# Attention core: in every second step one copy out of PSUM goes from VectorE to ScalarE

## The chip, the core and the metric

The kernel runs on one core of one Trainium2 chip. Its engines take part under the profile's names: PE is TensorE (matrix products, and transposes as products with the identity), PEld its weight loads, DVE is VectorE, ACT is ScalarE, POOL is GpSimd, SP issues transfers. The metric is the device time of one execution in microseconds (us); less is better.

## The reference, cut to what is computed

A backbone of two layers over 1024 latent tokens and 256 context tokens, width 1024. Layer 0 mixes with a Fourier transform and a state-space scan, layer 1 with differential attention; each layer ends in a squared-ReLU MLP. The change lies in the attention of layer 1, which has 8 heads, two score maps per head, and keys and values over all 1280 tokens:

```python
def diff_attend(q, k, v, lam):
    s = jnp.einsum("bqhmd,bkhmd->bhmqk", q, k).astype(F32) * (DA_HEAD_DIM ** -0.5)
    p = jax.nn.softmax(s, axis=-1)
    w = (p[:, :, 0] - lam * p[:, :, 1]).astype(v.dtype)
    return jnp.einsum("bhqk,bkhd->bqhd", w, v)
```

Queries are taken in blocks of 128 tokens, so that there are 8 heads times 8 blocks.

## The kernel before

Everything is in 32-bit floats. `attn_core` works through 64 items, one for each head and each block of 128 queries (`qt` counts the blocks). It is a software pipeline written out by hand: the loop over `i` issues in one step the work of up to five items at different stages, and every engine runs its own instructions in the order in which they are written. The names of the stages are those of the code: in step `i`, `cur` is item `i`, `last` is item `i-1`, `turned` is item `i-2`, `old` is item `i-3` and `done` is item `i-4`.

For item `cur`, `qk` (line 2002) computes on TensorE the scores of the first map into the PSUM tile `SC[0]` and of the second map into `SC[1]`, 128 x 1280 each, in six products each. `peak` (line 2007) takes each row's maximum on VectorE, `expo` (line 2013) the exponential with the row's sum on ScalarE, into the SBUF tiles `P` and `R`. For `last`, `combine` and `combine_tail` form first map plus factor times second map: VectorE makes the reciprocal (line 2020) and the factor, GpSimd the first 896 columns, VectorE the last 384. For `turned`, `turn` (lines 2033 to 2038) transposes the ten 128 x 128 tiles of the combined weights on TensorE through the PSUM tile `TB`, which holds four of them: first the tiles 8 and 9, then 4 to 7, then 0 to 3. After each of the three groups `TB` is copied into the SBUF tile `wT`. For `old`, `pv` (line 2042) multiplies the transposed weights with the values. For `done`, `store` scales the result and `power` (line 2051) takes its sum of squares.

There is one `TB`, one `SC[0]` and one `SC[1]`: `qk` of the next step overwrites what `expo` of this step reads. In a step TensorE's order is: scores of the first map, transposes 8 and 9, scores of the second map, transposes 4 to 7, half of `pv`, the other half, transposes 0 to 3. ScalarE's order is: copy 8 and 9, `power`, copy 4 to 7, first exponential, second exponential. VectorE's order is: reciprocal and factor, `store`, both maxima, tail of the combination, small operations from a list (`drip`, at most three in a step), copy 0 to 3.

Once per head, the output rows are normalized: `norm` puts some dozen small operations on the list, which lie in the steps with a number of 4 to 7 modulo 8, and `out` transposes the results through `TB` (four more transposes in steps with the number 0 and 1 modulo 8, with a copy by ScalarE, line 2085, and a cast by VectorE, line 2086, one step later). Towards the end of the core, splits of weight tiles (lines 349 and 353) are put behind the steps as well. Helpers such as line 312 and 340 record the operations of many places in the code, so that the tile's name tells which one it is.

Of the kernel before, what the change touches and what calls it, by code (L numbers as in the profile page):

```python
# [217 lines left out]
class Kern:  # L218
# [1763 lines left out]
    def attn_core(self, P, rest, more, tail):  # L1982
# [3 lines left out]
        p0r, p1r, s2 = P  # L1986
        cols = [(0, 512), (512, 512), (1024, 256)]
        f = lambda a: a.rearrange("p a b -> p (a b)")
        heads, items = self.heads, {}

        def begin(h, qt):
            if qt == 0:
                O = self.R.v(8, 128) if h + 1 < NH else self.Kr.v(8, 128).bitcast(F32)
                heads[h].update(O=O, t=s2.v(4, 8))
            it = items[h, qt] = dict(st=self.S.v(2, 8), P=[p0r.v(1280)])
            return it

        def qk(h, qt, i, part):
# [30 lines left out]
        def turn(it, c0):  # L2029
            m = min(4, 10 - c0)  # L2030
            ps = self.TB[:, :128 * m]
            for j in range(m):
                nc.tensor.transpose(ps[:, 128 * j:128 * j + 128],  # L2033
                                    it["P"][0][:, 128 * (c0 + j):128 * (c0 + j) + 128], self.ident)
            if c0:
                nc.scalar.copy(f(it["wT"][:, c0:c0 + m]), ps)
            else:
                nc.vector.tensor_copy(f(it["wT"][:, c0:c0 + m]), ps)
# [53 lines left out]
        for i in range(n + 5):  # L2092
# [5 lines left out]
            if cur:  # L2098
                h, qt = cur
                if i == 2:  # L2100
                    self.core_q(0, 1)
                if h + 1 < NH:
                    if qt == 3:
                        self.core_load(h + 1)
                    if qt == 4:
                        self.core_q(h + 1, 0)
                    if qt == 6:
                        self.core_q(h + 1, 1)
                it = begin(*cur)
                qk(*cur, 0, cols)  # L2110
                peak(it, 0)
            if turned:
                ti = items[turned]
                ti["wT"] = wr.v(10, 128)
                turn(ti, 8)
# [4 lines left out]
            if turned:  # L2120
                turn(ti, 4)
# [18 lines left out]
            if turned:  # L2140
                turn(ti, 0)
# [358 lines left out]
```

## Time and profile before

| | |
|---|---|
| time, median of 3 runs | 2878.57 us (2871.09 to 2879.25) |
| the profiled execution | 2877.97 us, span of its trace 2876.2 us |
| TensorE busy (PE) | 2782.5 us, 97% of the span |
| its weight loads (PEld) | 2327.5 us, 81% |
| VectorE busy (DVE) | 2030.6 us, 71% |
| ScalarE busy (ACT) | 1132.2 us, 39% |
| GpSimd busy (POOL) | 1517.7 us, 53% |
| copies of line 2038 (DVE) | 64, of 677 to 693 ns, from 1745.3 to 2123.9 us |
| copies of line 2036 (ACT) | 128, 64 of 256 columns and 64 of 512, of 372 to 587 ns |

The shares are means over stages that have different limits. Times in the views of the trace count from the span's start.

### The profile page before, as it was taken

Reading aid. Unit: us, or ns where it says so; the run is one execution under the profiler, and the core shown is the slowest. Engines: PE = TensorE matmul, PEld = TensorE weight load, DVE = VectorE, ACT = ScalarE, POOL = GpSimd, SP = SyncE. Lnnn points to the kernel's source line nnn. Section 1 sums busy time; section 2 is a strip of 40 time slices with the busy share of each in tenths; the row PEclk is TensorE's granted clock in tenths of the full one; section 3 lists DMA queues with packets and bytes.
Section 4 is the critical chain, followed back from the end, with each engine's and each line's share of the span. In section 5 each row is a group of like instructions: output and inputs, shape, how many; then the busy total and the mean of one; then the engine's idle time right before and its main releaser. Section 6 shows DMA issues by size and latency. Waiting matters only on the chain. (4 is left out here: it accounts for less than half of the span.)

```text
span 2876.2 us, 40633 instructions
## 1 busy us (share of the span) xinstructions
PE 2782.5 (97%) x14850; PEld 2327.5 (81%) x14850; DVE 2030.6 (71%) x3769; ACT 1132.2 (39%) x2036; POOL 1517.7 (53%) x1247
## 2 busy tenths in 40 slices
PE   5899999999999999999999999999999999999999
PEld 2666788788888888888778788999988888878887
DVE  7789867785654566668588848999977344347776
ACT  3341434444444311113334436666643545432220
POOL 5613313544444666665334426787733555577773
PEclk8899899999999999999999999999999999999999
DMA  7354540377777885854164643323222566589892
GB/s 288 103 171 170 184 147 15 124 259 247 258 245 260 264 263 169 252 180 117 52 205 120 161 123 90 104 78 94 72 96 74 205 220 224 208 290 287 256 263 81
DMA packets 308200, 504.59 MB, mean 175 GB/s; under 512 B 17569, under 2 KB 175777, under 8 KB 307489
## 3 DMA queue, kind: packets, MB, share of 16 engines
q1 hardware_dynamic: 235344, 355.18, 37.4%
q0 software_dynamic: 72656, 146.82, 17.2%
q8 instruction: 117, 1.92, 0.3%
q14 instruction: 83, 0.67, 0.1%
HBM read 332.56 MB, written 169.38 MB: 175 GB/s over the span
## 5 line engine op out<-in xcount | busy, mean ns | idle before, releaser
L353 POOL TENSOR_TENSOR W<-R,W 128x512 fp32r<-128x512 f32 (+1 forms) x181 | 323.9, 1797 | 433.6 <-ACT W L349 425.5
L357 PE MATMUL bank<-hl,W 128*128 128x512 f32 (+1 forms) x1224 | 479.3, 392 | 5.7 <-ACT hl L449 3.7
L358 PE MATMUL bank<-hl,W 128*128 128x512 f32 (+1 forms) x1224 | 474.5, 388 | 8.4 <-DVE hl L312 5.8
L359 PE MATMUL bank<-hl,W 128*128 128x512 f32 (+1 forms) x1224 | 471.8, 385 | 1.1 <-DVE W L353 1.1
L312 DVE SCALAR_TENSOR_TENSOR xL<-bank,k,xL 128x512 f32<-128x512 f32 x344 | 245.8, 745 | 103.2 <-PE bank L359 100.4
L349 ACT CAST W<-R 128x512 fp32r<-128x512 f32 (+2 forms) x237 | 184.9, 798 | 311.3 <-PE bank L359 135.5
L357 PEld LDWEIGHTS bank<-hl,W 128*128 128x128 f32 x1224 | 232.4, 190 | 72.1 <-issue 20.3
L358 PEld LDWEIGHTS bank<-hl,W 128*128 128x128 f32 x1224 | 232.5, 190 | 56.0 <-DVE hl L312 11.8
L359 PEld LDWEIGHTS bank<-hl,W 128*128 128x128 f32 x1224 | 231.8, 189 | 47.5 <-DVE W L353 1.5
L357 PE MATMUL bank<-oS,W 128*128 128x512 f32 x568 | 221.3, 390 | 0.5 <-DVE xL L312 0.5
L359 PE MATMUL bank<-oS,W 128*128 128x512 f32 x568 | 221.2, 389 | 0.0
L358 PE MATMUL bank<-oS,W 128*128 128x512 f32 x568 | 221.2, 389 | 0.0
L2007 DVE TENSOR_REDUCE S<-sc 128x1 f32<-128x1280 f32 x128 | 184.3, 1481 | 38.9 <-PE sc L2002 38.9
L353 POOL TENSOR_TENSOR W<-E,W 128x512 fp32r<-128x512 f32 x108 | 139.8, 1312 | 105.0 <-ACT W L349 104.7
L312 DVE SCALAR_TENSOR_TENSOR Y<-R,k,Y 128x256 f32<-128x256 f32 x224 | 159.8, 747 | 16.7 <-DMA R<-in_ada_w_dram 13.2
L2002 PE MATMUL sc<-K,W 128*128 128x512 f32 x720 | 168.1, 370 | 0.0
L340 POOL TENSOR_TENSOR R<-R,S 128x896 f32<-128x896 f32 x64 | 107.3, 1677 | 111.4 <-DVE S L312 85.2
L357 PE MATMUL bank<-hb,W 128*128 128x512 f32 x400 | 156.6, 392 | 3.1 <-DMA hb<-h_w 2.1
L2042 PE MATMUL pv<-xL,wT 128*128 128x128 f32 x1280 | 155.9, 275 | 0.0
L359 PE MATMUL bank<-hb,W 128*128 128x512 f32 x400 | 155.8, 390 | 0.0
L358 PE MATMUL bank<-hb,W 128*128 128x512 f32 x400 | 155.8, 390 | 0.0
L312 DVE TENSOR_TENSOR M<-bank,M 128x512 f32<-128x512 f32 x144 | 98.8, 691 | 80.5 <-PE bank L359 80.5
(422 smaller groups left out, 6977.6 us busy)
## 6 DMA issues: line engine op xcount, KB each, us to landing
h_w<-M SPq DMA_DIRECT2D x192, 512.0 KB, 3.5
hl<-h_w POOLq DMA_DIRECT2D x106, 512.0 KB, 6.9
oS<-h_w POOLq DMA_DIRECT2D x72, 512.0 KB, 7.4
R<-in_w_dram SPq DMA_DIRECT2D x64, 512.0 KB, 4.3
R<-in_w_dram SPq DMA_DIRECT2D x112, 256.0 KB, 5.1
R<-in_ada_w_dram SPq DMA_DIRECT2D x52, 512.0 KB, 5.0
h_w<-Y SPq DMA_DIRECT2D x36, 512.0 KB, 3.5
hb<-h_w POOLq DMA_DIRECT2D x34, 512.0 KB, 7.2
```

The source lines that it names most:

```text
L312: f(**kw)
L340: self.nc.gpsimd.tensor_tensor(out=o, in0=a, in1=b, op=op)
L349: nc.scalar.copy(hi, src)
L353: e.tensor_tensor(out=lo, in0=src, in1=hi.bitcast(F32), op=ALU.subtract)
L357: mm(ps, lhsT=lh, rhs=rh, start=first, stop=False)
L358: mm(ps, lhsT=lh, rhs=rl, start=False, stop=False)
L359: mm(ps, lhsT=ll, rhs=rh, start=False, stop=last)
L2002: nc.tensor.matmul(self.SC[i][:, c0:c0 + n], lhsT=Qf[:, e, q0:q0 + 128], rhs=K[:, i, c0:c0 + n], start=e == 0, stop=e == 1)
L2007: nc.vector.tensor_reduce(out=st[:, i, 1:2], in_=self.SC[i][:, 0:1280], axis=AX.X, op=ALU.max, negate=True)
L2042: nc.tensor.matmul(self.PV[:, 0:128], lhsT=it["wT"][:, kt], rhs=heads[h]["v"][:, kt], start=kt == 8, stop=kt == 3)
```

## The change

`turn` is called three times for an item, with `c0` = 8, 4 and 0. So far the copies for 8 and 4 are ScalarE's and that for 0 (tiles 0 to 3, the last four) is VectorE's. With the change the item carries a mark whether its number `qt` within the head is even, and for such items the last copy too is written for ScalarE. Since eight blocks make a head, these are the items with an even number, and they are `turned` in the steps with an even number. The place in the code where the copy is issued stays the same: after the second half of `pv` and before the second exponential.

```diff
-            it = items[h, qt] = dict(st=self.S.v(2, 8), P=[p0r.v(1280)])
+            it = items[h, qt] = dict(st=self.S.v(2, 8), P=[p0r.v(1280)], even=qt % 2 == 0)
...
-            if c0:
+            if c0 or it["even"]:
                 nc.scalar.copy(f(it["wT"][:, c0:c0 + m]), ps)
             else:
                 nc.vector.tensor_copy(f(it["wT"][:, c0:c0 + m]), ps)
```

## Rows read from the trace of the kernel before

**Rows 1.** Busy table of one stretch: us, PE, PEld, DVE, ACT, POOL, clock, DMA.
```profile
1892.00:1939.00 47.00, 46.82 (x345) 43.32 (x344) 45.51 (x70) 32.19 (x67) 37.09 (x24) 1.00 0.28 87
```

**Rows 2.** Groups by line, 1800 to 2080 us: busy us, mean ns, idle before, releasers.
```profile
L2038 DVE COPY wT<-tb 128x512 f32<-128x512 f32 x47 | 32.2, 685 | 5.4 <-PE tb L2033 5.2 <-ACT R L2013 0.3
```

**Rows 3.** Waits, 1800 to 2080 us: waiting line, releaser, total us, times, longest.
```profile
ACT wT L2036 <- PE tb L2033: 73.7, 78, 1.3
...
PE tb L2033 <- DVE wT L2038: 1.4, 7, 0.3
```

**Rows 4.** Timeline of steps 22 and 23 (6 and 7 modulo 8): start, us, instruction.
```profile
1859.98 0.60 PE L2033 MATMUL tb<-k,P 128*128 128x128 f32 x4
...
1860.47 0.15 DVE L312 TENSOR_TENSOR s<-s 128x8 f32<-128x8 f32 x1
...
1860.94 0.69 DVE L2038 COPY wT<-tb 128x512 f32<-128x512 f32 x1
...
1861.54 0.16 DVE L2020 RECIPROCAL S<-S 128x2 f32<-128x2 f32 x1
...
1861.87 1.43 PE L2002 MATMUL sc<-K,W 128*128 128x512 f32 x6
...
1862.13 2.88 DVE L2007 TENSOR_REDUCE S<-sc 128x1 f32<-128x1280 f32 x2
...
1863.13 0.60 PE L2033 MATMUL tb<-k,P 128*128 128x128 f32 x4
...
1863.77 0.59 ACT L2036 COPY wT<-tb 128x512 f32<-128x512 f32 x1 [0.94 <-PE tb L2033]
...
1864.25 1.33 ACT L2013 ACTIVATE P<-sc,S 128x1280 f32<-128x1280 f32 x1
1864.93 1.43 DVE L312 SCALAR_TENSOR_TENSOR P<-R,S,P 128x384 f32<-128x384 f32 x1
...
1865.57 1.33 ACT L2013 ACTIVATE R<-sc,S 128x1280 f32<-128x1280 f32 x1
...
1865.80 0.60 PE L2033 MATMUL tb<-k,P 128*128 128x128 f32 x4
...
1866.28 0.15 DVE L312 TENSOR_TENSOR s<-s 128x8 f32<-128x8 f32 x1
...
1866.55 0.69 DVE L2038 COPY wT<-tb 128x512 f32<-128x512 f32 x1
```

**Rows 5.** Timeline at steps 20, 26 and 28 (4, 2 and 4 modulo 8).
```profile
1848.08 0.60 PE L2033 MATMUL tb<-k,P 128*128 128x128 f32 x4
...
1883.90 0.60 PE L2033 MATMUL tb<-k,P 128*128 128x128 f32 x4
...
1885.64 1.42 PE L2002 MATMUL sc<-K,W 128*128 128x512 f32 x6
...
1895.28 0.60 PE L2033 MATMUL tb<-k,P 128*128 128x128 f32 x4
...
1896.49 0.68 DVE L2038 COPY wT<-tb 128x512 f32<-128x512 f32 x1
...
1897.23 0.44 PE L2033 MATMUL tb<-k,P 128*128 128x128 f32 x2 [0.18 <-DVE wT L2038]
...
1897.42 1.42 PE L2002 MATMUL sc<-K,W 128*128 128x512 f32 x6
```

**Rows 6.** Timeline at the core's start, in steps 1 and 2.
```profile
1739.11 1.33 ACT L2013 ACTIVATE R<-sc,S 128x1280 f32<-128x1280 f32 x1
...
1740.56 0.17 DVE L2020 RECIPROCAL S<-S 128x2 f32<-128x2 f32 x1 [6.55 <-ACT R L2013]
1740.58 1.43 PE L2002 MATMUL sc<-K,R 128*128 128x512 f32 x6 [0.65 <-ACT R L2013]
```

**Rows 7.** Timeline at step 60, near the core's end.
```profile
2085.87 0.60 PE L2033 MATMUL tb<-k,P 128*128 128x128 f32 x4
...
2088.43 1.41 PE L2002 MATMUL sc<-K,W 128*128 128x512 f32 x6
```

## The prediction

> **What bounds the kernel now.** Only the attention core is touched: 64 steps, eight of which take 47.2 us (1848.08 to 1895.28) [rows 5], some 378 of 2876 us. So I read the busy table by stretch for it first. Over about one head TensorE works 46.82 of 47 us, VectorE 45.51 and ScalarE 32.19, at a granted clock of 1.00, the level of 2.4 GHz [rows 1]. Two engines are near full and the third has 14.8 us to spare in eight steps: on shares alone, a VectorE copy goes to the engine with room. The second view, the groups by line, prices that copy: 685 ns, nearly always behind something else [rows 2]. The third, the list of waits, says what VectorE's fullness costs TensorE between 1800 and 2080 us: TensorE waits for this copy 7 times, 1.4 us in all, while ScalarE stands idle for the transposes 73.7 us [rows 3]. So TensorE sets the pace, and VectorE overruns it only now and then. The view that decides is the fourth, the timeline: not how much room ScalarE has, but where in the step it lies.
>
> I measure from T0, the start of the last four transposes of a step, to the start of the next step's second score product, which I call S1. From S1 back to the next T0 is 3.93 us (1861.87 to 1865.80) in the steps without the output's transposes [rows 4], and the change touches nothing in it. So each step's length changes by what T0 to S1 changes. That interval is now 1.74 us where TensorE runs unhindered (1883.90 to 1885.64), 2.14 where the first small normalization operations of a head sit before VectorE's copy (1895.28 to 1897.42) [rows 5], and 1.89 where the next ones do (1859.98 to 1861.87) [rows 4]. By the step number modulo 8 these are steps 2, 4 and 6; step 5 has the same small operations as 6, step 7 has two of them, and 0, 1 and 3 I take as unhindered.
>
> **The change, part by part.** *Removed:* in even steps VectorE no longer makes the copy, which holds its queue for 0.60 us (1860.94 to 1861.54, where the reciprocal begins) [rows 4].
>
> *Added:* the same copy stands in ScalarE's queue. The copy of four other transposed tiles has its form: it holds the queue for 0.48 us (1863.77 to 1864.25) [rows 4]. By busy time that is nothing.
>
> *Where it stands:* the queue runs in written order, and the copy is written between the first and the second exponential. Now the second exponential follows the first at once: 1864.25, 1865.57, that is 0.23 us before T0 at 1865.80 [rows 4]. With the copy ahead of it, it can't. The copy needs the transposes, and ScalarE's copy of four tiles starts 0.64 us after their transposes start (1863.13 to 1863.77) [rows 4]. So copy at T0 + 0.64, second exponential at T0 + 1.12. It is 1.35 us later than now. Queued behind it are the exponential, and for that wait S1 on TensorE (it overwrites the scores that the exponential reads; there is one buffer of each of the two score tiles) and the reciprocal on VectorE.
>
> *What the exponential lets go:* at the start of the core both releases are bare. It started at 1739.11; the reciprocal began at 1740.56 and the score product at 1740.58 [rows 6]: 1.45 and 1.47 us later. So in an even step S1 comes at T0 + 1.12 + 1.47 = T0 + 2.59, against 1.74, 2.14 or 1.89 now. TensorE's loss is 0.85 us in steps 0 and 2, 0.45 in step 4, 0.70 in step 6: 2.85 us per eight steps. Its work in order behind S1 has no other cover: nothing else is queued that could go first.
>
> *VectorE after that:* the reciprocal comes at T0 + 2.57, then VectorE needs 3.39 us to the mixing of the two tails (1861.54 to 1864.93) and 1.35 to what follows (1866.28) [rows 4]. In the odd step its own copy thus starts at T0 + 7.31 + d, d being the small operations ahead of it: 0.47 us for three (1860.47 to 1860.94), 0.27 for two (1866.28 to 1866.55) [rows 4]. The copy frees the transposes' bank after 0.74 us and S1 follows 0.19 us later (1896.49, 1897.23, 1897.42) [rows 5]: S1 at T0 + 8.24 + d. TensorE's own T0 of the odd step is at T0 + 2.59 + 3.93 = 6.52, so the odd step's T0 to S1 is 1.72 + d, or 1.74 if that is more. Step 3: 1.74, no change. Step 5: 2.19 instead of 1.89, 0.30 more. Step 7: 1.99 instead of some 1.74, 0.25 more. Step 1 has a cast ahead of the copy, but four more transposes on TensorE in the step before hide it: no change. Odd steps add 0.55 us.
>
> *Does the delay go on to the first exponential?* It needs the first maximum, which ends 0.59 + 1.48 after the reciprocal (1861.54, 1862.13, two maxima 2.88 us) [rows 4]: T0 + 4.72 with 0.08 to pass it on. ScalarE comes to it at S1 + 1.90 + 0.48 (1861.87, 1863.77, 1864.25) [rows 4], T0 + 4.97. It is covered by 0.25 us, so I cost it at nothing; without that cover it would be paid one for one at the next first score product.
>
> *Sum.* Eight steps cost 2.85 + 0.55 = 3.40 us more. Steps 10 to 57 are six times eight: 20.4 us. Steps 2 to 9 have no small operations yet, so the four even ones cost 0.85 each: 3.4. At the end (58, 60, 62) splits of weights lie in both queues. Step 58 I cost as the others, 0.85; in step 60 the interval is already 2.56 (2085.87 to 2088.43) [rows 7], so it costs nothing; step 62 lies between nothing and 0.85, and I take 0.35, nearer to step 60, which has the same company. Step 64 has no exponential behind the copy. Together 25.0 us. The profiled execution took 2877.97 us beside a span of 2876.2, and is 0.6 us below the median: 2877.97 + 25.0 = **2903.0 us**, 0.85% more than the median.
>
> The row of scores says that one buffer per score tile lets a late exponential hit TensorE within the same step [rows 6]. The Trainium skill (Perfetto Trace Analysis, Optimizing Tensor Performance, Matmuls) wants independent groups of products rotated through different PSUM banks, so that emptying one overlaps the next. By that rule, with a second pair of score tiles, the delay of 1.35 us would meet a spare step and the sum would be only VectorE's relief, some -5 us; by the rows there is no such pair, and it is +25.
>
> **The rivals.** *Relief wins.* VectorE is the bound, and taking 0.60 us from it in every second step shortens the core. For it: VectorE is busy 45.51 of 47 us [rows 1], and steps 4 and 6 do wait for it. The Trainium skill (Perfetto Trace Analysis, Optimizing Scalar/DVE Operations) says that moving work to ScalarE may make sense where VectorE is saturated. As a mechanism here: even steps fall to 1.74, 0.40 us less in step 4 and 0.15 in step 6, 0.55 per eight steps, 3.3 us for six times eight, and some 0.8 in step 60: 2874 us. That is within 0.3%, so even this rival would hardly be seen. Against it: it decides only where T0 to S1 is over 2.59 us now, and none of the intervals above is. Chance 0.05.
>
> *VectorE is late too, and the delay goes on.* The cover of 0.25 us before the first exponential is thin; if the reciprocal, or the split of a weight behind the later exponential, comes 0.5 us later than I have it, 0.25 us goes through to TensorE in each of 31 even steps, about 8 us: 2911. Chance 0.17.
>
> *The second exponential frees its scores sooner.* The releases of 1.47 us rest on bare starts only [rows 6]. If the product went on at the end of the exponential itself (1.33 us), each even step would pay 0.14 less, 31 times, 4 us; and if odd steps didn't wait for VectorE, 3 to 4 us less again: 2895. Chance 0.13.
>
> *The change does nothing:* ScalarE's copy is hidden in its idle time, S1 stays put. That needs the exponential to stay ahead of T0, which the written order excludes unless the order isn't kept; 2878, chance 0.02.
>
> **How the numbers follow.** Forecast as worked out, 2898 to 2908: 0.63. The range of 8 in 10 runs from 2893 to 2912, which takes in the cheaper and dearer variants and leaves out relief, no effect and a little on either side. About 0.3% is what a measurement of this kernel tells from no change, 8.6 us. Relief ends inside that band, or just beyond if it is larger: faster 0.02, the same 0.05, slower 0.93.
>
> **What would show it.** Right: ScalarE's second exponential starts some 1.1 us after T0 in even steps and 0.2 before it in odd ones; TensorE waits for it some 0.4 to 0.9 us at S1, about 30 times, a wait that the list doesn't have now; VectorE's reciprocal waits for ScalarE in even steps; eight steps take near 50.6 us instead of 47.2; all other stages keep their lengths. Wrong: no wait of TensorE for the second exponential, or a core that gets shorter; or a wait at the first score product as well, which would be the dearer rival.

## The result and the profile after

The change makes the kernel slower: 2897.01 us (median of 6 runs, 2895.71 to 2902.61) against 2873.76 us for the kernel before in the same comparison, a ratio of 1.0083 with a 95% interval of 1.0068 to 1.0098. That is 23 us. The forecast was 25.0 us more, and 2903.0 us in all; of the 6 us between 2903.0 and 2897.0, 4.2 are that the sum started from an execution of 2877.97 us while the kernel before came out at 2873.76 with more runs, and 1.8 that the loss is 23.25 us.

The profiled execution took 2902.54 us beside a span of 2900.7 us, 24.5 us more than the span before. Where do they lie? The view of one line shows when it first and last ran. The products with the values (line 2042) run from the first to the last item of the core. Before:

```profile
L2042 PE MATMUL pv<-xL,wT x1280: 270/276/276, 1748.0 to 2131.0; 128*128 128x128 f32 x183
```

and after:

```profile
L2042 PE MATMUL pv<-xL,wT x1280: 270/275/367, 1746.8 to 2154.9; 128*128 128x128 f32 x183
```

383.0 us have become 408.1, 25.1 us more: the whole loss is in the attention core, and the rest of the program is 0.6 us shorter. Its busy table after the change, for a stretch of about one head (columns as in [rows 1]), shows both full engines with room:

```profile
1894.00:1944.00 50.00, 47.20 (x343) 42.99 (x342) 43.02 (x65) 34.05 (x70) 37.10 (x23) 1.00 0.25 81
```

TensorE is busy 47.20 of 50 us where it was 46.82 of 47 [rows 1], and VectorE 43.02. The work was lifted from a full engine, and now none is full: the sign of a new wait. The list of waits after the change names it (1740 to 2160 us, the whole core, as for the lists below where no other stretch is named; waiting line, releaser, total us, times, longest):

```profile
ACT wT L2036 <- PE tb L2033: 103.3, 116, 3.7
...
DVE S L2020 <- ACT R L2013: 46.2, 28, 2.4
PEld sc L2002 <- ACT R L2013: 26.0, 31, 0.9
PE sc L2002 <- ACT R L2013: 18.5, 30, 0.6
...
PE tb L2033 <- DVE wT L2038: 3.0, 8, 0.9
```

TensorE's score product waits for ScalarE's second exponential in 30 of the 31 even steps that have a following one (all but step 2), its weight loads in all 31. Before the change this wait occurs once, at the core's start [rows 6], and not between 1800 and 2080 us. VectorE's reciprocal waits for the same exponential, 46.2 us in all. The timeline after the change, at an even step and the odd one behind it (steps 22 and 23, as in [rows 4]), shows the wait at its place:

```profile
1866.87 0.60 PE L2033 MATMUL tb<-k,P 128*128 128x128 f32 x4
...
1867.51 0.58 ACT L2036 COPY wT<-tb 128x512 f32<-128x512 f32 x1 [0.77 <-PE tb L2033]
1867.99 1.33 ACT L2013 ACTIVATE R<-sc,S 128x1280 f32<-128x1280 f32 x1
...
1869.21 0.20 ACT L2013 ACTIVATION_READ_ACCUMULATOR R<-sc,S 128x1 f32 x1
...
1869.44 0.17 DVE L2020 RECIPROCAL S<-S 128x2 f32<-128x2 f32 x1 [1.52 <-ACT R L2013]
...
1869.47 1.43 PE L2002 MATMUL sc<-K,W 128*128 128x512 f32 x6 [0.63 <-ACT R L2013]
...
1873.16 1.33 ACT L2013 ACTIVATE R<-sc,S 128x1280 f32<-128x1280 f32 x1
...
1873.40 0.60 PE L2033 MATMUL tb<-k,P 128*128 128x128 f32 x4
...
1874.47 0.69 DVE L2038 COPY wT<-tb 128x512 f32<-128x512 f32 x1
...
1875.22 0.44 PE L2033 MATMUL tb<-k,P 128*128 128x128 f32 x2
...
1875.41 1.42 PE L2002 MATMUL sc<-K,W 128*128 128x512 f32 x6
```

With T0 at 1866.87 the copy starts at T0 + 0.64, the second exponential at T0 + 1.12, the reciprocal at T0 + 2.57 and S1 at T0 + 2.60. Between the exponential and what it lets go stands the read of its row's sum, 0.20 us. ScalarE was idle for 0.77 us ahead of the copy, waiting for the transposes, with the exponential's scores ready behind it. In the odd step the exponential starts 0.24 us before T0, as it did before the change in steps 3 to 58 (0.17 us in those with the output's transposes).

### The profile page after: what moved, and what is told of

Same layout as the page of the kernel before. It is cut to its first block, busy times and chain, and to the rows that moved or that the text cites. A ratio compares the mean times of both kernels' runs of the same rounds, so it can differ in the third digit from the quotient of the medians.

```text
span 2900.7 us, 40632 instructions
## 1 busy us (share of the span) xinstructions
PE 2785.1 (96%) x14850; PEld 2325.1 (80%) x14850; DVE 2013.4 (69%) x3737; ACT 1150.5 (40%) x2068; POOL 1520.0 (52%) x1247
## 3 DMA queue, kind: packets, MB, share of 16 engines
q8 instruction: 117, 1.92, 0.3%
## 4 chain that ended last, share of the span: by engine, by line
PE 38%; DVE 7%; issue 2%; ACT 2%; POOL 1%; DMA 1%; SPq 0%; POOLq 0%; DVEq 0%; ACTq 0%
PE bank L357 10%; PE bank L358 10%; PE bank L359 10%; DVE S L2007 3%; PE pv L2042 2%; PE sc L2002 2%; DVE P L312 1%; ACT R L2013 1%; PE sc L358 1%; PE sc L359 1%; PE tb L2033 1%; PE sc L357 1%; PE bank L1877 1%; POOL R L340 1%; DVE S L312 1%
## 5 line engine op out<-in xcount | busy, mean ns | idle before, releaser
L2002 PEld LDWEIGHTS sc<-K,W 128*128 128x128 f32 x720 | 126.2, 189 | 46.7 <-ACT R L2013 25.6
```

The costliest lines, as they stand in the source:

```text
L2002: nc.tensor.matmul(self.SC[i][:, c0:c0 + n], lhsT=Qf[:, e, q0:q0 + 128], rhs=K[:, i, c0:c0 + n], start=e == 0, stop=e == 1)
```

## The experiments

Two theories stood against each other at first. **Queue order:** what costs is that the copy, which waits for the transposes, stands ahead of the second exponential; the same work elsewhere in ScalarE's queue would cost nothing. **Load:** ScalarE's added work, or its reading of that bank, costs wherever it stands. A third, **VectorE**, asks whether VectorE's relief or its later start carries part of the result. The core's length below is taken as above, from the first to the last product with the values; it was 383.0 us before the change and 408.1 after.

**The copy behind the exponential.** The same 32 copies stay on ScalarE, written one place later:

```diff
+            if not c0 and it["even"]:
+                return
...
             if cur:
                 expo(it, 1)
+            if turned and ti["even"]:
+                nc.scalar.copy(f(ti["wT"][:, 0:4]), self.TB)
```

> The same 32 copies on ScalarE, but written behind the second exponential instead of ahead of it. Queue-order theory: the second exponential starts before T0 again, the copy runs at about T0 + 1.08, frees the transposes' bank at T0 + 1.7 and S1 comes at about T0 + 1.9 in even steps (now 2.6), so the loss of 23 us goes away: within 3 us of the kernel before. TensorE's wait for the second exponential is gone from the list. Rival, load: ScalarE's added work, or its reading of that bank, costs wherever it stands: still some 20 us slower than before.

Measured: 2871.90 us against 2872.94, ratio 0.9993 (0.9982 to 1.0003); core 382.2 us. The timeline of step 28 in this kernel:

```profile
1891.35 1.33 ACT L2013 ACTIVATE R<-sc,S 128x1280 f32<-128x1280 f32 x1
...
1891.59 0.60 PE L2033 MATMUL tb<-k,P 128*128 128x128 f32 x4
...
1892.65 0.59 ACT L2147 COPY wT<-tb 128x512 f32<-128x512 f32 x1
...
1893.30 0.44 PE L2033 MATMUL tb<-k,P 128*128 128x128 f32 x2
...
1893.49 1.41 PE L2002 MATMUL sc<-K,W 128*128 128x512 f32 x6
```

The exponential is ahead of T0 again (1891.59) and S1 comes at T0 + 1.90. The work is the same and the loss is gone: the load theory falls. Step by step the copy isn't free here either: steps 0 and 2 take 0.17 to 0.19 us longer than before the change, and VectorE's relief gives it back in steps 3 to 5.

**The copy on ScalarE in every step.** The dose doubled:

```diff
-            if c0:
+            if True:
                 nc.scalar.copy(f(it["wT"][:, c0:c0 + m]), ps)
```

> ScalarE makes the last copy in all 64 items, ahead of the second exponential. Queue-order theory: every step now has S1 at T0 + 2.59, so 0.85 us more in steps 0 to 3 and 7 modulo 8, 0.45 in step 4, 0.70 in 5 and 6, 6.1 per eight steps; with the first and last steps some 45 us slower than before (1.6%), about twice the change. About 61 waits of TensorE for the second exponential. Rival, VectorE: what costs in the changed kernel is VectorE's late start in the odd steps; with no copy left on VectorE the loss shrinks below 24 us.

Measured: 2918.09 us against 2872.94, ratio 1.0159 (1.0145 to 1.0173), 45 us; core 428.6 us, 45.6 more than before. From step 3 to step 62 T0 to S1 is 2.60 us, and 2.65 in steps with the output's transposes. Its list of waits:

```profile
DVE S L2020 <- ACT R L2013: 84.7, 56, 2.3
PEld sc L2002 <- ACT R L2013: 51.0, 61, 0.9
PE sc L2002 <- ACT R L2013: 36.4, 60, 0.6
```

Twice the copies, twice the waits. VectorE has no such copy left and waits 84.7 us at its reciprocal, so its late start in odd steps isn't what the loss is mainly made of.

**Early transposes.** The copy stays where the change put it, ahead of the second exponential, in even steps without the output's transposes. What it waits for comes earlier:

```diff
+            outed = len(ready) > 0
+            if turned and outed:
+                ti["even"] = False
...
+            soon = turned and not outed and ti["even"]
+            if soon:
+                turn(ti, 0)
             if old:
                 pv(old[0], items[old], (7, 0, 1, 2, 3))
-            if turned:
+            if turned and not soon:
                 turn(ti, 0)
```

> ScalarE makes the last copy in even steps other than those with the output's transposes (step 0 modulo 8 stays on VectorE), ahead of the second exponential as in the change, but TensorE issues the transposes between the two halves of the product with the values, 1.1 us earlier. Queue-order theory: ScalarE finds them finished when the first exponential is done, so the copy holds the queue for 0.48 us and doesn't wait; the second exponential starts 0.48 us later than before instead of 1.35, and S1 is let go just when TensorE comes to it (5.64 us after the last S1, TensorE's own step being 5.67): within 4 us of the kernel before. Rival, load or place in the queue as such: some 17 us slower, three quarters of the change.

Measured: 2873.94 us against 2872.94, ratio 1.0007 (0.9998 to 1.0016); core 382.8 us. The timeline of one such step (22, from 1852.99 on), with the odd step before it:

```profile
1850.77 0.60 PE L2033 MATMUL tb<-k,P 128*128 128x128 f32 x4
...
1852.06 0.68 DVE L2038 COPY wT<-tb 128x512 f32<-128x512 f32 x1
...
1852.80 0.44 PE L2033 MATMUL tb<-k,P 128*128 128x128 f32 x2 [0.28 <-DVE wT L2038]
...
1852.99 1.41 PE L2002 MATMUL sc<-K,W 128*128 128x512 f32 x6
...
1855.36 1.33 ACT L2013 ACTIVATE P<-sc,S 128x1280 f32<-128x1280 f32 x1
1855.79 0.60 PE L2033 MATMUL tb<-k,P 128*128 128x128 f32 x4
...
1856.67 0.59 ACT L2036 COPY wT<-tb 128x512 f32<-128x512 f32 x1
1857.14 1.35 ACT L2013 ACTIVATE R<-sc,S 128x1280 f32<-128x1280 f32 x1
...
1858.63 1.43 PE L2002 MATMUL sc<-K,W 128*128 128x512 f32 x6
```

The copy starts 1.31 us behind the first exponential, with no idle time shown before it, and S1 follows the last S1 by 5.64 us. So being ahead of the exponential isn't what cost the 23 us; being ahead of it while still waiting for transposes is. Being ahead without a wait isn't free, though. VectorE's reciprocal, behind the later exponential, comes just ahead of S1, and VectorE's own copy is late in the odd steps as it is in the change: T0 to S1 is 2.22 us in step 21 (1850.77 to 1852.99), against 1.89 to 1.92 in steps 5 modulo 8 before. From one S1 to the next, steps 4 and 6 take 5.64 us instead of 6.05 and 5.82, and steps 5 and 7 take 6.15 and 5.95 instead of 5.83 and 5.66 (medians). The relief is there in the even steps, and the odd ones take it back.

**VectorE not relieved.** The change, with a sum on VectorE in the place of each copy that it gave away (its result is used by nothing):

```diff
                 nc.scalar.copy(f(it["wT"][:, c0:c0 + m]), ps)
+                if not c0:
+                    w = f(it["wT"][:, 4:8])
+                    nc.vector.tensor_tensor(out=self.E.v(512), in0=w, in1=w, op=ALU.add)
```

> The change, and VectorE makes an added sum of 128 x 512 from SBUF (0.7 us, result unused) where its copy was in even steps, so that it is relieved of nothing. Queue-order theory: in even steps VectorE waits 1.3 to 2.4 us for the second exponential's sum, so the added work is hidden: 23 us slower than before, within 4 us of the change. Rival: the relief of VectorE paid back a good part of the loss in the changed kernel; without it the loss grows to 35 to 43 us.

Measured: 2901.66 us against 2872.94, ratio 1.0102 (1.0086 to 1.0118); core 408.5 us, where the change has 408.1. By the medians it is 5.5 us more than the change's 23.3, but the two intervals overlap and the core is as long, so I read no cost out of it. Its list of waits:

```profile
PEld sc L2002 <- ACT R L2013: 26.1, 31, 0.9
DVE S L2020 <- ACT R L2013: 25.1, 28, 1.5
PE sc L2002 <- ACT R L2013: 19.2, 31, 0.7
```

The reciprocal's wait falls from 46.2 to 25.1 us, by 21.1 us, about what 31 sums of 0.68 us take. TensorE's wait stays, and T0 to S1 is 2.60 us in the even steps as in the change (2.65 in step 0). In the change, then, VectorE's relief only became waiting.

**The odd items instead of the even ones.**

```diff
-            it = items[h, qt] = dict(st=self.S.v(2, 8), P=[p0r.v(1280)], even=qt % 2 == 0)
+            it = items[h, qt] = dict(st=self.S.v(2, 8), P=[p0r.v(1280)], even=qt % 2 == 1)
```

> The change in the odd items instead of the even ones: the same number of copies moved, in other steps. Queue-order theory with the step-by-step sum: 0.85 us in steps 1, 3 and 7, 0.70 in step 5, and in the even steps VectorE now comes 0.3 us late in 4, 6 and 2: 4.15 per eight steps instead of 3.40, some 28 us slower than before, 4 to 5 more than the change. Rival, load: the same 23 us as the change.

Measured: 2904.86 us against 2874.97, ratio 1.0107 (1.0093 to 1.0120), 30 us; core 413.1 us, 30.1 more than before and 5.0 more than the change. The intervals of the two ratios overlap a little (the change: 1.0068 to 1.0098), so it is the steps that decide: eight of them take 51.4 us here, 4.2 more than before, where the change has 50.6. The timeline of steps 28 and 30 in this kernel, where VectorE makes the copy:

```profile
1903.00 0.60 PE L2033 MATMUL tb<-k,P 128*128 128x128 f32 x4
...
1905.26 0.44 PE L2033 MATMUL tb<-k,P 128*128 128x128 f32 x2 [0.51 <-DVE wT L2038]
1905.45 1.42 PE L2002 MATMUL sc<-K,W 128*128 128x512 f32 x6
...
1915.91 0.60 PE L2033 MATMUL tb<-k,P 128*128 128x128 f32 x4
...
1918.12 1.40 PE L2002 MATMUL sc<-K,W 128*128 128x512 f32 x6
```

T0 to S1 is 2.45 and 2.21 us; before the change it was 2.14 and 1.89 in these steps [rows 4, 5]. So the second part of the mechanism is seen by itself here: VectorE, held at the reciprocal by the late exponential, brings its own copy 0.3 us later in the next step.

**A version that beats both.** Early transposes and ScalarE's copy in all steps without the output's transposes (in those VectorE keeps it), and as a control the same early transposes with every copy left as before:

```diff
-            it = items[h, qt] = dict(st=self.S.v(2, 8), P=[p0r.v(1280)])
+            it = items[h, qt] = dict(st=self.S.v(2, 8), P=[p0r.v(1280)], even=True)
...
-            if c0:
+            if c0 or it["even"]:
```

> As the experiment with the early transposes, in all steps but those with the output's transposes (0 and 1 modulo 8, where VectorE keeps the copy). Queue-order theory: no wait of TensorE for the second exponential, and VectorE has 0.6 us less in the steps in which it was late: 0.40 us gained in step 4, 0.15 in 5 and 6, some 2 us at the end, 4 to 8 us faster than the kernel before (0.15 to 0.3%). Rival, load: slower, by 30 us or more (three quarters of 64 copies).

> Control: the transposes early in the same steps, but all copies as in the kernel before, on VectorE. If the place of the transposes alone did something, it would show here. Expected: within 2 us of the kernel before, since TensorE's work in a step is the same and VectorE comes to the copy at the same time.

Measured: 2870.69 us against 2874.97, ratio 0.9987 (0.9978 to 0.9996), core 378.4 us, 4.6 less than before. The control: 2874.57 us against 2874.97, ratio 0.9997 (0.9988 to 1.0006), core 383.9 us. Of the waits of TensorE's products between 1800 and 2100 us the first of these kernels has left:

```profile
PE tb L2033 <- DVE wT L2038: 0.5, 1, 0.5
PE tb L2033 <- ACT E L2085: 0.5, 1, 0.5
```

Before the end of the core no product waits for the second exponential; there the weight loads ahead of the score products do so three times, 0.2 us each.

This is VectorE's relief, obtained: 4 us, 0.13%. Eight steps take 46.39 us (T0 at 1844.43 in step 20, at 1890.82 in step 28) instead of 47.20; of the 2 us expected at the end only 0.3 came (steps 58 to 62). The place of the transposes alone gives nothing, as the control shows. Neither do early transposes with the copy on ScalarE in even steps only, the experiment above, where 25 copies moved and eight steps took 47.19 us. Here 50 moved, the odd steps' among them, and VectorE has no copy left in steps 2 to 7 modulo 8 that could be late. All copies written behind the exponential would be the other way to the same relief; that wasn't run.

## Why the prediction was right

The mechanism held step by step. That the sum met the core's 25.1 us to a tenth is partly luck: of its three parts two were too high and one too low. T0 to S1 by step, modulo 8, in us; before, as forecast, and after (one instance each):

| step | before | forecast | after | times of T0 and S1 after |
|---|---|---|---|---|
| 0 | 1.79 | 2.59 | 2.65 | 1879.84, 1882.49 |
| 1 | 1.80 | 1.74 | 1.80 | 1886.93, 1888.73 |
| 2 | 1.74 | 2.59 | 2.60 | 1892.64, 1895.24 |
| 3 | 1.79 | 1.74 | 1.73 | 1899.18, 1900.91 |
| 4 | 2.14 | 2.59 | 2.60 | 1904.82, 1907.42 |
| 5 | 1.89 | 2.19 | 2.21 | 1860.75, 1862.96 |
| 6 | 1.89 | 2.59 | 2.60 | 1866.87, 1869.47 |
| 7 | 1.75 | 1.99 | 2.01 | 1873.40, 1875.41 |

- *The release of 1.47 us*, which rested on two bare starts [rows 6], held: S1 comes 1.48 us behind the second exponential's start in every even step from 4 to 62 (1867.99, 1869.47 in the timeline above).
- *S1 to T0 unchanged at 3.93 us*: 1869.47 to 1873.40. The cover of 0.25 us before the first exponential held up to step 60; in steps 61 and 63 the first exponential does wait for the maximum, 0.24 and 0.23 us, and no product waits for it. The first score product waits for an exponential only once, 0.7 us at the core's start, as before the change.
- *Eight steps*, forecast 47.2 + 3.40 = 50.6 us, took 50.61 (T0 at 1854.21 in step 20, at 1904.82 in step 28). From T0 of step 10 to T0 of step 58, 283.63 us became 303.69: 20.1 more, against 20.4 in the sum. Steps 38 and 56 were already long before (2.24 and 2.23 us), which the sum didn't know.
- *The first steps* were priced too high: 3.4 us taken, 2.8 measured (T0 of step 2 to T0 of step 10, 46.61 before and 49.42 after). The sum took step 2 as unhindered. It isn't: there the first score product waits for the first exponential, so T0 to S1 is 3.15 us before the change and 3.11 after, and ScalarE's copy costs nothing. Before:

```profile
1743.12 0.66 PE L2033 MATMUL tb<-k,P 128*128 128x128 f32 x4 [0.68 <-ACT wT L2036]
...
1744.44 1.43 PE L2002 MATMUL sc<-K,R 128*128 128x512 f32 x6 [0.66 <-ACT P L2013]
...
1746.27 1.41 PE L2002 MATMUL sc<-K,R 128*128 128x512 f32 x6
```

and after:

```profile
1741.99 0.66 PE L2033 MATMUL tb<-k,P 128*128 128x128 f32 x4 [0.68 <-ACT wT L2036]
...
1745.10 1.44 PE L2002 MATMUL sc<-K,R 128*128 128x512 f32 x6
```

- *The end* was priced too low: 1.2 us taken, 2.1 measured (T0 of step 58 to T0 of step 63, 31.68 before and 33.80 after). Step 62 pays 0.66 instead of 0.35 (1.99 before, 2.65 after), and step 61, taken as free, pays 0.61 (1.90 before, 2.51 after). Steps 58 and 60 came as forecast (2.60 and 2.59). What the sum left out is that a split of a weight starts on ScalarE behind the later exponential, and VectorE's part of it, which waits for ScalarE's, stands ahead of the reciprocal. So the reciprocal comes late, and with it VectorE's copy in step 61:

```profile
2111.24 0.42 DVE L353 TENSOR_TENSOR W<-R,W 128x256 fp32r<-128x256 f32 x1 [1.15 <-ACT W L349]
2111.59 0.16 DVE L2020 RECIPROCAL S<-S 128x2 f32<-128x2 f32 x1
...
2114.90 0.60 PE L2033 MATMUL tb<-k,P 128*128 128x128 f32 x4
...
2117.22 0.44 PE L2033 MATMUL tb<-k,P 128*128 128x128 f32 x2 [0.57 <-DVE wT L2038]
2117.41 1.41 PE L2002 MATMUL sc<-K,W 128*128 128x512 f32 x6
```

- *The rival that relief wins* failed for the reason given: in the even steps T0 to S1 was nowhere over 2.59 us before, but in step 2, where the copy decides nothing. The filled VectorE shows that the relief was worth nothing in the change. The 4 us of the last version are close to the 4 us at which this rival was priced, but not by its sum, which moved the even copies alone: with those, early transposes gained nothing. (Beside the second pair of score tiles the prediction calls the same relief some -5 us; its own sum is 4.1.)
- *VectorE's cost to TensorE before the change* was read too low, which no term of the sum used. The 1.4 us [rows 3] are the products' waits for the copy; the weight loads of the same transposes wait more, and their row, between 1800 and 2080 us as well, is nearer to what the last version gained:

```profile
PEld tb L2033 <- DVE wT L2038: 4.3, 15, 0.5
```

- *The dearer rival* (VectorE late by more, the delay going on to the first exponential) didn't occur. Its cause, a split that comes late, did, but only at the end, and TensorE paid for it through VectorE's copy in step 61. Nor did *the cheaper one* (S1 let go at the exponential's own end, 1.33 us).

The prediction weighed two rules of the Trainium skill. By the first (Perfetto Trace Analysis, Optimizing Tensor Performance, Matmuls) independent products rotate through different PSUM banks. No run here had a second pair of score tiles, so its number stays untested; that one buffer passes a late exponential on to TensorE is what the runs show. By the second (Perfetto Trace Analysis, Optimizing Scalar/DVE Operations) moving work from a full VectorE to ScalarE may make sense. In these runs it cost 0.83% where the moved copy waited in ScalarE's queue, changed nothing where it didn't wait and 25 or 32 copies were moved, and gained 0.13% with 50.

## What to carry to other kernels

An engine's idle share says that work fits, not where: ask at which place of its queue the moved instruction is written, what it waits for there, and which instruction behind it was ready sooner. Here 0.48 us of work held an exponential back by 1.35 us, and TensorE paid. The remedy is as cheap as the fault: write the instruction behind the urgent one, or let what it waits for come earlier, and look whether the wait has gone before judging the move. Then look at the neighbouring step: moving half of the copies gave nothing even without the wait, because the other half came later.

## What the runs showed of the hardware

One thing I hadn't expected: VectorE's added sum of 128 x 512 out of SBUF took 677 to 691 ns in 27 of its 32 places, and 1522 to 1527 ns in the other five. In each of the five GpSimd's instruction of the same size on the output rows (`R<-R,s`) had started 0.37 to 0.39 us earlier (once at 1879.89, with the sum at 1880.27). It took 1.35 to 1.37 us there, as it does in the change without the sums. In six other places VectorE's sum started first, 0.08 to 0.16 us ahead of another GpSimd instruction of that size (`oS<-E,oS`). There the sum kept its 677 to 680 ns, and GpSimd's took 1.65 to 1.73 us, where the same instruction takes 1.28 to 1.30 elsewhere in this run. So of two such instructions the one that starts later was the slower one each time; the runs don't show why.
